# One layer of a hybrid SSD and S5 encoder: angle tables made per batch, another form of the S5 GELU, and a new order of the instructions

## The chip, the cores and the metric

The kernel runs on one core of a Trainium2 chip. The time is the device time of one execution in microseconds (us). Work goes to five engines, each with its own queue of instructions that it works through in order: TensorE (PE, matrix products), VectorE (DVE), ScalarE (ACT, functions through tables), GpSimd (POOL) and SyncE (SP), which here only starts transfers.

## What is computed

One inference step of one layer, for 1024 prompt frames and 32 frames of a running stream with its own states. Both share one set of weights; the width is 1024.

```python
xn = rmsnorm(x, pre_mix_norm_w)
z, xbc, dt_raw, u_s5 = split(xn @ w_in)                  # 512 | 1024 | 8 | 512 columns
y_ssd = ssd_mixer(z, xbc, dt_raw, ...)                   # causal conv, SiLU, chunked scan, gate, norm
# s5_mixer: 32 groups of 16 channels, each a diagonal complex state of 64
dt = exp(log_dt); ang = lam_im * dt; mag = exp(lam_re * dt)
lb = mag * (cos(ang) + i sin(ang))                       # the step of the scan
h  = associative_scan(lb, B u, start=h0)
y  = Re(C h) + d * u
g  = gelu(y, approximate=True) @ glu_w + glu_b           # per group
y_s5 = g[..., :16] * sigmoid(g[..., 16:])
h  = x + rmsnorm(concat(y_ssd, y_s5) @ w_out, post_mix_norm_w)
up = causal_dwconv(rmsnorm(h, pre_ffn_norm_w) @ w_up)    # 5632 columns
gate, val = split(up)
y  = h + rmsnorm((gelu(gate) * val) @ w_down, post_ffn_norm_w)
```

Outputs are y and the new states and conv histories of both streams, in float32.

## The kernel before

The 1056 columns (frames) lie in the free dimension, the features on the 128 partitions. Block 0 is 512 columns, block 1 is 544, worked in two chunks of 272. The large products are made of three passes in a reduced format that together carry the accuracy of float32: high weight by high input, high weight by low input, low weight by high input (`pm` is the PSUM tile). Weights come as tiles of 128 by 1024 (`raw`, 512 KB each). For each, ACT writes the high part (`wh`, line 566, which is the line of a helper that holds all of ACT's operations), and DVE the rest (`wl`, line 745). Two buffers each hold `raw`, `wh` and `wl`. The line of nearly all matmuls is 510, of the transposes 514.

The stages: the first norm (its per-column factor is made by a chain of small DVE operations, lines 634 to 657, on tiles `nrt`, `nry`, `nra`; it is spread over the partitions through `scr` and a product with ones), the projection `w_in`, then SSD and S5 side by side with the stream of weights, `w_out`, and the feed-forward part: `up_evac` reads PSUM into `fext` (lines 1771 and 1773, DVE), the convolution and GELU follow, and the second product collects in `acc` (line 1843). At the end of each block, `fin_mm` and `fin_out` make the last norm. `apply` (lines 1932 to 1946) treats a chunk in four pairs of 128-feature rows: each is multiplied by the norm's factor (line 1939, `acc<-acc,sacc`) and the residual is added (line 1945 from `hr` in block 0, line 1942 from `o` in block 1). The tuple `fp` names, per chunk, the pairs whose multiplication (and, for block 0 and the first chunk of block 1, addition) goes to POOL instead of DVE.

S5 goes in 8 batches of four groups; a column there is 132 slots of 8 frames each (528 elements for four groups). For each batch:

- `s5_prep` makes products of parameters on POOL (`outer`, line 1129: `gz`, `gt` and the W tiles; `gz` is the sum of two products, line 1134). PE uses `gz` in a product with `ck`, whose result goes through DRAM to `Traw` and `Tg`, and in transposes, which ACT copies to `GT`. It also makes the angle tables TC (cosine) and TS (sine) of the slots: ACT scales the slot numbers to turns, DVE takes off whole turns (lines 1143 to 1146, and `wrap`, 931 and 932), ACT takes Sin. Two batches share this: the even batch (`u == 0`) makes the turns for both, one batch on each half of the partitions, in `yr`; each batch takes Sin on its half and sends the copies to the other half by three transfers.
- `s5_run` makes the input products, turns them with TC and TS into `rr`, scans (R), and turns back into `hq` (line 1212 on POOL, 1213 on DVE).
- `s5_out` makes the output product of three terms in PSUM, its GELU by the tanh formula (Copy and Square from PSUM on ACT, an operation on DVE, Tanh on ACT, an operation on DVE), and the GLU.

ACT holds one set of function tables at a time: by the kernel's own list, Silu and Sin are in one, Gelu_apprx_tanh in another, Exp in a third; where the set changes, an ACT_TABLE_LOAD stands in its queue.

The order of the instructions on each engine is set ahead of the run by a class `Plan`. It reads all instructions and what each depends on (`read`, `buffers`), gives each a duration (`cost`), and makes a list schedule: on each engine, of those that are ready, the one of the best rank comes first (`schedule`). Ranks come from `ROUND` passes backward and forward (`rounds`), then each seed in `NUDGES` shifts the ranks of some instructions in a stretch at random, one after the other (`nudge`). The orders of the last pass are fixed with dependencies. So a new constant or a new seed can move any instruction of any engine.

## Time and profile before

| what | us |
|---|---|
| median of three runs | 1260.25 |
| range of the three runs | 1259.05 to 1261.12 |
| the profiled execution | 1260.22 |
| its span, first to last instruction | 1258.4 |
| busy: PE, DVE, ACT, POOL | 1225.7, 1004.5, 573.0, 409.1 |
| mean granted PE clock, share of full speed | 0.980 |
| first matmul starts, last one ends | 1.24, 1250.3 |

Busy time says how full an engine is. A wait on PE shows as idle time in front of an instruction, and its releaser is the instruction of another engine that ended it. The clock that PE is granted is given as a share of 2.4 GHz; at 0.50 every matmul takes twice as long.

### The profile page before, as it was taken

What the parts mean: (1) busy time and instruction counts of PE and PEld (TensorE: products, weight loads), DVE (VectorE), ACT (ScalarE), POOL (GpSimd) and SP (SyncE); (2) the same over time, 40 slices, a digit from 0 to 9 for tenths busy, and PEclk for the clock granted to TensorE, in tenths of its full rate; (3) what the DMA queues carried; (4) which work ended last, traced back from release to release, by engine and by line L of the source; (5) the groups of instructions that cost most, each with busy time, mean ns of one, the idle gap of its engine ahead of it and who ended that gap; (6) DMA issues with size and microseconds to landing.
All of it is one profiled execution on the core that took longest, in us unless ns stands there. A gap on an engine that the chain in (4) does not pass through costs nothing.

```text
span 1258.4 us, 20994 instructions
## 1 busy us (share of the span) xinstructions
PE 1225.7 (97%) x7885; PEld 1105.9 (88%) x7885; DVE 1004.5 (80%) x1755; ACT 573.0 (46%) x967; POOL 409.1 (33%) x574
## 2 busy tenths in 40 slices
PE   9999999999998999999999999998999999999995
PEld 7879989998887887878987888898999999999994
DVE  6788877898979898887698987778676777776777
ACT  8246655564545554543454433362532333333343
POOL 3484555363156333221453311126110111111013
PEclk7899989999999999999999999999999999999997
DMA  7154434243346322333433432223322232322212
GB/s 242 39 156 128 117 87 133 82 125 103 100 125 205 117 93 76 117 131 108 137 112 102 142 101 87 98 85 125 110 85 84 84 101 85 101 85 84 85 54 72
DMA packets 68821, 135.39 MB, mean 108 GB/s; under 512 B 14320, under 2 KB 35184, under 8 KB 68720
## 3 DMA queue, kind: packets, MB, share of 16 engines
q1 hardware_dynamic: 68720, 134.05, 34.0%
q8 instruction: 62, 1.02, 0.3%
q14 instruction: 39, 0.32, 0.1%
HBM read 111.69 MB, written 15.81 MB: 101 GB/s over the span
## 4 chain that ended last, share of the span: by engine, by line
PE 84%; DVE 5%; issue 1%; DMA 1%; ACT 1%; POOL 0%; SPq 0%; DVEq 0%; ACTq 0%; POOLq 0%
PE pm L510 75%; PE ms L510 9%; PE ms L514 1%; DVE o L1707 1%; DVE wl L745 1%; DVE acc L1939 0%; DMA raw<-wt 0%; DVE xl L1710 0%; ACT L566 0%; DMA kd<-s5d 0%; SPq L1190 0%; DVE acc L1942 0%; DVE sp L1335 0%; DMA gluw<-glu 0%; DVE acc L1945 0%
## 5 line engine op out<-in xcount | busy, mean ns | idle before, releaser
L510 PE MATMUL pm<-xh,wh 128*128 128x272 f32 (+1 forms) x1616 | 527.6, 329 | 3.5 <-DVE fext L1771 2.2
L510 PE MATMUL pm<-xh,wl 128*128 128x272 f32 (+1 forms) x1616 | 526.4, 329 | 4.1 <-DVE wl L745 4.1
L510 PE MATMUL pm<-xl,wh 128*128 128x272 f32 (+1 forms) x1616 | 527.5, 327 | 2.0 <-DVE xl L1710 1.9
L510 PEld LDWEIGHTS pm<-xh,wh 128*128 128x128 f32 x1616 | 306.6, 190 | 26.8 <-issue 3.1
L510 PEld LDWEIGHTS pm<-xh,wl 128*128 128x128 f32 x1616 | 305.6, 190 | 27.7 <-DVE wl L745 5.3
L510 PEld LDWEIGHTS pm<-xl,wh 128*128 128x128 f32 x1616 | 306.9, 190 | 24.2 <-DVE xl L1710 2.3
L566 ACT ACTIVATE wh<-raw 128x1024 fp32r<-128x1024 f32 x120 | 126.6, 1056 | 153.8 <-PE pm L510 133.1
L510 PE MATMUL pm<-al,dh 128*128 128x272 f32 (+1 forms) x528 | 170.4, 325 | 0.0
L510 PE MATMUL pm<-ah,dh 128*128 128x272 f32 (+1 forms) x528 | 169.3, 326 | 1.0 <-ACT acc L566 0.8
L510 PE MATMUL pm<-ah,dl 128*128 128x272 f32 (+1 forms) x528 | 168.3, 323 | 0.0
L745 DVE TENSOR_TENSOR wl<-raw,wh 128x1024 fp32r<-128x1024 f32 x120 | 157.5, 1314 | 13.4 <-ACT wh L566 13.0
L1843 DVE TENSOR_TENSOR acc<-acc,pm 128x272 f32<-128x272 f32 (+1 forms) x232 | 119.2, 521 | 51.0 <-PE pm L510 49.5
L1788 DVE SCALAR_TENSOR_TENSOR ftmp<-fext,vec_t,ftmp 128x512 f32<-128x512 f32 (+1 forms) x176 | 141.3, 804 | 13.1 <-ACT ftmp L566 11.1
L1766 POOL COPY fext<-halo 128x2 f32<-128x2 f32 x88 | 41.9, 476 | 298.7 <-DVE ftmp L1788 281.2
L1771 DVE TENSOR_TENSOR fext<-pm,rbc 128x512 f32<-128x512 f32 (+2 forms) x132 | 67.2, 511 | 74.4 <-PE pm L510 73.5
L566 ACT ACTIVATE ftmp<-fext,vec_t 128x512 f32<-128x512 f32 (+1 forms) x88 | 72.4, 824 | 83.3 <-DVE fext L1773 40.3
L510 PEld LDWEIGHTS pm<-ah,dh 128*128 128x128 f32 x528 | 99.0, 188 | 9.1 <-ACT acc L566 1.0
L510 PEld LDWEIGHTS pm<-al,dh 128*128 128x128 f32 x528 | 99.3, 188 | 7.2 <-issue 0.3
L510 PEld LDWEIGHTS pm<-ah,dl 128*128 128x128 f32 x528 | 98.6, 188 | 7.3
L566 ACT ACTIVATE dh<-raw 128x1024 fp32r<-128x1024 f32 (+1 forms) x46 | 46.7, 1020 | 75.1 <-PE pm L510 62.5
L1821 DVE TENSOR_TENSOR dl<-raw,dh 128x1024 fp32r<-128x1024 f32 (+1 forms) x46 | 56.7, 1235 | 7.1 <-ACT dh L566 7.1
L566 ACT ACTIVATE ftmp<-ftmp 128x512 f32<-128x512 f32 (+1 forms) x44 | 28.1, 639 | 70.9 <-DVE ftmp L1788 70.9
(323 smaller groups left out, 1659.0 us busy)
## 6 DMA issues: line engine op xcount, KB each, us to landing
raw<-wt SPq DMA_DIRECT2D x164, 512.0 KB, 3.3
gluw<-glu SPq DMA_DIRECT2D x8, 512.0 KB, 3.6
xst<-xT SPq DMA_DIRECT2D x16, 136.0 KB, 3.2
pbd<-pbo SPq DMA_DIRECT2D x8, 272.0 KB, 2.5
xr<-xT SPq DMA_DIRECT2D x8, 272.0 KB, 3.1
pbi<-pbd SPq DMA_DIRECT2D x8, 272.0 KB, 2.9
yT<-acc SPq DMA_DIRECT2D x8, 272.0 KB, 2.2
ud<-uext SPq DMA_DIRECT2D x4, 528.0 KB, 2.9
```

Of the source, the lines that this page charges most:

```text
L510: PE.matmul(out, lhsT, rhs, start=start, stop=stop, **kw)
L514: PE.transpose(out, in_, ident)
L566: S.activation(out, in_, func, bias=bias, scale=scale)
L745: V.tensor_tensor(lo, r, hi.bitcast(F32), sub)
L1707: V.scalar_tensor_tensor(h, h, vc("post_mix", k), r1, mult, mult)
L1766: G.tensor_copy(e[:, 0:2], halo[:, j, :])
L1771: V.tensor_tensor(e[:, 2 + o:2 + o + wp], ps[:, :wp], rbc[:, t0:t0 + wp], mult)
L1788: V.scalar_tensor_tensor(t, e[:, i:i + n], vc("fw", 3 * j + i), t, mult, add)
L1821: V.tensor_tensor(l, rr, h.bitcast(F32), sub)
L1843: V.tensor_tensor(a, a, ps[:, :w], add)
```

## The change

Four parts.

1. The angle tables are made batch by batch, on all 128 partitions: turns, wrap, Sin for TS, Abs and Sin for TC. The three transfers per batch, the constant `nsgn2pi` and four small copies into `dt5` go. Per pair of batches there are now 8 scaled copies, 4 Sins and 2 Abs on ACT (before 4, 5 and 1), and twice as many operations for turns and wrap on DVE.
2. The GELU of the S5 output is one ACTIVATE, Gelu_apprx_tanh from PSUM. Two ACT operations and two DVE operations of each batch go in part or whole: both Copies, both Squares and the Tanh on ACT become two Gelus, and the two DVE operations are gone. The factor 2 that the tanh form left in is taken out of the GLU's scales (0.25 becomes 0.5).
3. `fp` gives one pair of the first chunk of block 1 back to DVE.
4. In `cost` three estimates change, and ROUND and NUDGES are new (ROUND 7 with 33 seeds, now 6 with 56).

In the order of the changed kernel there are 7297 matmuls as before, 1771 DVE operations (before 1757), 974 on ACT (969), among these 35 table loads (22), 577 on POOL (579), and 481 transfers (505).

```diff
 PAR = dict(...
-           fp=((1, 3), (1, 3), ()),
+           fp=((1, 3), (3,), ()),
...
-ROUND, NUDGES = 7, (12, 19, 34, 43, 47, 57, 66, 73, 88, 96, 149, 160, 173, 180, 187, 210, 250, 257, 276, 376, 383,
+ROUND, NUDGES = 6, (14, 35, 47, 59, 82, 112, 125, 149, 188, 206, 225, 233, 269, 353, 368, 418, 536, 595, 612, 651,
...
         elif e == "Pool":
             self.shared[q] = len(big) > 1
-            d = 0.21 + 0.00165 * n if len(big) > 1 else 0.17 + 0.0009 * n
+            d = 0.21 + 0.0021 * n if len(big) > 1 else 0.17 + 0.0009 * n
         else:
-            self.shared[q] = not ps and n > 8
+            self.shared[q] = not ps
...
-                wire = max(wire, s + 0.9) + self.bytes[q] / 280e3
+                wire = max(wire, s + 0.9) + self.bytes[q] / 380e3
...
-        for k, n in enumerate(("f8a", "f8b")):
-            for hf in range(2):
-                q = slice(64 * hf, 64 * hf + 64)
-                V.tensor_copy(dt5[q, 16 * k:16 * k + 16].rearrange("p (i g) -> p i g", g=4),
-                              small[n][q].rearrange("p (i h g) -> p i h g", h=2, g=4)[:, :, hf])
...
-        if u == 0:
-            yy = small["yy"] = tl("tytr", [128, 2, 4, NCH5], "yr")
-            y, t = yy[:, 0], yy[:, 1]
-            f8 = small["dt5"]
-            for g in range(4):
-                act(y[:, g], cs("slot"), AF.Copy, scale=f8[:, 2 * i + g:2 * i + g + 1])
-            V.tensor_scalar(t, y, MAGIC, MAGIC, add, sub)
-            V.tensor_tensor(y, y, t, sub)
-            for g in range(4):
-                V.scalar_tensor_tensor(y[:, g], cs("slot"), f8[:, 16 + 2 * i + g:17 + 2 * i + g], y[:, g], mult, add)
-            wrap(y, t)
-            act(t, y, AF.Abs)
-            act(t, t, AF.Sin, scale=-TWOPI, bias=cs("halfpi"))
-        y, t = small["yy"][:, 0], small["yy"][:, 1]
-        me, other = (slice(64 * v, 64 * v + 64) for v in (u, 1 - u))
-        act(TSn[me], y[me], AF.Sin, scale=cs("sgn2pi")[me])
-        act(y[me], y[me], AF.Sin, scale=cs("nsgn2pi")[me])
-        D.dma_start(TSn[other], y[me])
-        D.dma_start(TC[me], t[me])
-        D.dma_start(TC[other], t[me])
+        y = tl("tytr", [128, 4, NCH5], "yr")
+        for g in range(4):
+            act(y[:, g], cs("slot"), AF.Copy, scale=small["f8a"][:, 4 * i + g:4 * i + g + 1])
+        V.tensor_scalar(TC, y, MAGIC, MAGIC, add, sub)
+        V.tensor_tensor(y, y, TC, sub)
+        for g in range(4):
+            V.scalar_tensor_tensor(y[:, g], cs("slot"), small["f8b"][:, 4 * i + g:4 * i + g + 1], y[:, g], mult, add)
+        wrap(y, TC)
+        act(TSn, y, AF.Sin, scale=cs("sgn2pi"))
+        act(y, y, AF.Abs)
+        act(TC, y, AF.Sin, scale=-TWOPI, bias=cs("halfpi"))
...
-        sq = th
...
-            act(y[:, 2 * b:2 * b + 2], pv, AF.Copy)
-            act(sq[:, 2 * b:2 * b + 2], pv, AF.Square)
-        V.scalar_tensor_tensor(sq, sq, 1.0 / GC1, y, add, mult)
-        act(th, sq, AF.Tanh, scale=GC0 * GC1)
-        V.scalar_tensor_tensor(gg, th, 1.0, y, add, mult)
+            act(gg[:, 2 * b:2 * b + 2], pv, AF.Gelu_apprx_tanh)
...
-                act(th[:, k], ps[1][:, o], AF.Tanh, scale=0.25, bias=gb_t[:, 4 * i + k, 1:2])
-                act(yq[:, k], ps[0][:, o], AF.Identity, scale=0.25, bias=gb_t[:, 4 * i + k, 0:1])
+                act(th[:, k], ps[1][:, o], AF.Tanh, scale=0.5, bias=gb_t[:, 4 * i + k, 1:2])
+                act(yq[:, k], ps[0][:, o], AF.Identity, scale=0.5, bias=gb_t[:, 4 * i + k, 0:1])
```

In the listings of the order the lines of the changed kernel differ from those of before: 1129 and 1134 became 1125 and 1130, 1212 became 1199, 1939, 1942 and 1945 became 1921, 1924 and 1927, 1771 became 1753, and the lines of the small chain and of `wl` are one higher.

POOL, near 165 us, where an S5 batch is prepared (`gz`, `gt`) while the batch ahead runs (`hq`, `fin`); `xb` and `o` are small copies of the SSD part. Before:

```order
L818 COPY o_73<-xb_90 128x3
L804 COPY xb_90<-xb_89 128x3
L1212 TENSOR_TENSOR hq<-R_1855,TS 128x4x132
L1215 COPY fin_107<-hq 128x4x4
L1216 COPY hq<-sml 128x8
L1129 TENSOR_TENSOR gz<-pq,bb 128x512
L1134 TENSOR_TENSOR gz<-gz,gt 128x512
L1129 TENSOR_TENSOR gt_2067<-pq,bcr 128x512
```

and now:

```order
L819 COPY o_73<-xb_90 128x3
L805 COPY xb_90<-xb_89 128x3
L1125 TENSOR_TENSOR gz<-pq,bb 128x512
L1130 TENSOR_TENSOR gz<-gz,gt 128x512
L1125 TENSOR_TENSOR gt_2053<-pq,bcr 128x512
L1199 TENSOR_TENSOR hq<-R_1846,TS 128x4x132
L1202 COPY fin_107<-hq 128x4x4
L1203 COPY hq<-sml 128x8
```

The pair of `gz` operations and a `gt` stood behind `hq` and its two copies, and now stand ahead of them.

DVE, near 870 us, where block 0 ends (`acc` is its result, `hr` the residual) and the feed-forward part of block 1 has begun (`fext` reads PE's result, `wl` is the low part of the next weights). Before:

```order
L1939 TENSOR_TENSOR acc_4899<-acc_4899,sacc 128x1024
L1771 TENSOR_TENSOR fext<-pm,rbc 128x272
L1945 TENSOR_TENSOR acc_4899<-acc_4899,hr 128x512 x2
L1771 TENSOR_TENSOR fext<-pm,rbc 128x240
L1771 TENSOR_TENSOR fext<-pm,rbc 128x272
L1771 TENSOR_TENSOR fext<-pm,rbc 128x240
L745 TENSOR_TENSOR wl<-raw,wh 128x1024
L1939 TENSOR_TENSOR acc_4899<-acc_4899,sacc 128x1024
L1945 TENSOR_TENSOR acc_4899<-acc_4899,hr 128x512
L745 TENSOR_TENSOR wl<-raw,wh 128x1024
L1773 TENSOR_TENSOR fext<-pm,rbc 128x32 x2
```

and now:

```order
L1770 SCALAR_TENSOR_TENSOR ftmp<-fext,vec_t,ftmp 128x546 x2
L1780 TENSOR_TENSOR ftmp<-ftmp 128x546
L1753 TENSOR_TENSOR fext<-pm,rbc 128x272
L1753 TENSOR_TENSOR fext<-pm,rbc 128x240
L1921 TENSOR_TENSOR acc_4883<-acc_4883,sacc 128x1024
L1927 TENSOR_TENSOR acc_4883<-acc_4883,hr 128x512 x2
L1755 TENSOR_TENSOR fext<-pm,rbc 128x32
L1753 TENSOR_TENSOR fext<-pm,rbc 128x272
L746 TENSOR_TENSOR wl<-raw,wh 128x1024
L1921 TENSOR_TENSOR acc_4883<-acc_4883,sacc 128x1024
L1927 TENSOR_TENSOR acc_4883<-acc_4883,hr 128x512 x2
```

Before, one `fext` read of 272 columns stood ahead of the first two additions and three reads behind them; now a read of 272 and one of 240 stand ahead of the multiplication and its additions, and the next three follow behind a `wl`.

DVE, at the very end: the applications of the pairs of the first chunk of block 1 (`acc` with `sacc`, `acc` with `o`) and the chain of the last norm. Before:

```order
L1907 TENSOR_TENSOR sacc<-sacc,osq 128x272
L1939 TENSOR_TENSOR acc_8893<-acc_8893,sacc 128x2x272
L1942 TENSOR_TENSOR acc_8893<-acc_8893,o_6246 128x2x272
L634 TENSOR_SCALAR nrt<-ms_13121 128x2
L634 TENSOR_SCALAR nrt<-ms_13121 16x1
L637 TENSOR_SCALAR nry<-nrt 128x3
L651 TENSOR_TENSOR nra<-nry 128x3
L652 SCALAR_TENSOR_TENSOR nra<-nra,nrt 128x3
L653 SCALAR_TENSOR_TENSOR nry<-nra,nry 128x3
L1939 TENSOR_TENSOR acc_8893<-acc_8893,sacc 128x2x272
```

and now:

```order
L1889 TENSOR_TENSOR sacc<-sacc,osq 128x272
L1921 TENSOR_TENSOR acc_8877<-acc_8877,sacc 128x2x272
L1924 TENSOR_TENSOR acc_8877<-acc_8877,o_6230 128x2x272
L635 TENSOR_SCALAR nrt<-ms_13105 128x2
L1921 TENSOR_TENSOR acc_8877<-acc_8877,sacc 128x2x272
L1924 TENSOR_TENSOR acc_8877<-acc_8877,o_6230 128x2x272
L635 TENSOR_SCALAR nrt<-ms_13105 16x1
L638 TENSOR_SCALAR nry<-nrt 128x3
L652 TENSOR_TENSOR nra<-nry 128x3
L653 SCALAR_TENSOR_TENSOR nra<-nra,nrt 128x3
```

Before, one pair stood ahead of the chain and half of another within it; now two pairs stand ahead of it, with one of the chain's operations between them.

## Rows read from the trace of the kernel before

**Rows 1.** Page, busy time of each engine (us, share of the span, instructions).

```profile
PE 1225.7 (97%) x7885; PEld 1105.9 (88%) x7885; DVE 1004.5 (80%) x1755; ACT 573.0 (46%) x967; POOL 409.1 (33%) x574
```

**Rows 2.** Waits of PE: waiting line, releaser, us in total, times, longest.

```profile
PE pm L510 <- DVE wl L745: 4.1, 3, 1.8
PE pm L510 <- DVE fext L1771: 2.2, 1, 2.2
PE pm L510 <- DVE xl L1710: 1.9, 1, 1.9
PE ms L510 <- POOL gz L1134: 1.9, 1, 1.9
...
PE pm L510 <- ACT wh L566: 1.1, 2, 0.7
```

**Rows 3.** Windows: length, busy PE, PEld, DVE, ACT, POOL, then clock, DMA, GB/s.

```profile
168.20:175.00 6.80, 6.55 (x24) 5.97 (x25) 4.99 (x9) 2.88 (x6) 2.83 (x4) 0.50 0.62 183
...
874.70:878.20 3.50, 3.50 (x18) 3.50 (x18) 3.47 (x5) 0.00 (x0) 3.50 (x5) 0.51 0.60 184
```

**Rows 4.** Windows, 100 to 300 us in four parts: busy us, the sum.

```profile
sum 200.00, PE 197.49 PEld 182.42 DVE 168.44 ACT 119.30 POOL 103.37; mean PE 49.37 PEld 45.60 DVE 42.11 ACT 29.82 POOL 25.84
```

**Rows 5.** ACT by form, 75 to 300 us: busy us, mean ns, idle before, releasers.

```profile
L566 ACT ACT_TABLE_LOAD x8 | 10.3, 1283 | 0.1
...
L566 ACT ACTIVATE y5s<-ms 128x264 f32<-128x264 f32 x16 | 6.3, 391 | 20.1 <-PE ms L510 19.6 <-DVE sp L1335 0.5
...
L566 ACT ACTIVATE ge<-ge 128x528 f32<-128x528 f32 x8 | 5.1, 642 | 2.1 <-DVE ge L1239 2.1
...
L566 ACT ACTIVATE yr<-cst_t,sml 128x132 f32<-128x132 f32 x12 | 4.3, 398 | 6.6 <-issue 4.2 <-DMA ug<-ud 2.1 <-DMA TS<-yr 0.3
```

**Rows 6.** Timeline of ACT (start, length, engine, line, operation, names, shapes).

```profile
105.11 1.28 ACT L566 ACT_TABLE_LOAD   x1
106.41 0.65 ACT L566 ACTIVATE ge<-ge 128x528 f32<-128x528 f32 x1
```

**Rows 7.** DVE by form, 75 to 300 us.

```profile
L1239 DVE SCALAR_TENSOR_TENSOR ge<-ge,y5s 128x528 f32<-128x528 f32 x8 | 8.8, 1096 | 3.6 <-ACT ge L566 3.6
L1241 DVE SCALAR_TENSOR_TENSOR ge<-ge,y5s 128x528 f32<-128x528 f32 x8 | 7.3, 913 | 0.1
...
L1168 DVE TENSOR_TENSOR kd<-kd 32x64 f32<-32x64 f32 x8 | 2.7, 336 | 3.2 <-DMA TS<-yr 1.7 <-DMA TC<-yr 0.7 <-DMA raw<-wt 0.4
```

**Rows 8.** Timeline of POOL, 160 to 172 us (in brackets: idle before, releaser).

```profile
162.47 1.33 POOL L1212 TENSOR_TENSOR hq<-R,TS 128x528 f32<-128x528 f32 x1 [2.73 <-ACT y5s L566]
...
165.68 1.05 POOL L1129 TENSOR_TENSOR gz<-pq,bb 128x512 f32<-128x512 f32 x1
166.81 1.59 POOL L1134 TENSOR_TENSOR gz<-gz,gt 128x512 f32<-128x512 f32 x1
```

**Rows 9.** Timelines of POOL, DVE and PE, 68 to 82 us.

```profile
71.54 1.29 POOL L1134 TENSOR_TENSOR gz<-gz,gt 128x512 f32<-128x512 f32 x1
...
68.77 4.22 DVE L1146 SCALAR_TENSOR_TENSOR yr<-cst_t,sml,yr 128x132 f32<-128x132 f32 x4
...
73.50 0.96 PE L510 MATMUL ms<-ck,gz 128*128 128x16 f32 x8
...
78.34 0.61 PE L510 MATMUL ms<-ug,GT 128*128 128x132 f32 x4
```

**Rows 10.** Timeline of DVE, 868 to 880 us.

```profile
867.66 4.23 DVE L1945 TENSOR_TENSOR acc<-acc,hr 128x512 f32<-128x512 f32 x2
```

**Rows 11.** Timelines of DVE and PE, the last 22 us.

```profile
1241.42 1.74 DVE L1942 TENSOR_TENSOR acc<-acc,o 128x544 f32<-128x544 f32 x1
...
1245.88 1.18 DVE L653 SCALAR_TENSOR_TENSOR nry<-nra,nry 128x3 f32<-128x3 f32 x1
...
1247.80 0.16 DVE L655 SCALAR_TENSOR_TENSOR nra<-nra,nrt 128x3 f32<-128x3 f32 x1
...
1249.00 1.27 PE L510 MATMUL ms<-scr,ones_r 128*128 128x272 f32 x2 [7.04 <-DVE scr L670]
```

More of the change, by code (lines that the diff above doesn't have):

```diff
@@ L50 @@
            run3=0.5, uload=6.619, swap_pool=1, z_s5=1, ssd0=13.784, ssd1=0.0, ssd2=2.778, gate0=76.032, glu0=0.384, glu1=2.807, abufs=2,
-           cvat='run7', tcat=1, late_at=2, nsq=1, fg=(), fp=((1, 3), (1, 3), ()), fch=(0, (0, 1), 2), pfin=0, q0=0, q1=0, q2=0, nb=0,
+           cvat='run7', tcat=1, late_at=2, nsq=1, fg=(), fp=((1, 3), (3,), ()), fch=(0, (0, 1), 2), pfin=0, q0=0, q1=0, q2=0, nb=0,
            hv=(), av=(3,), post0=0.802, dn_at=((3, 0), (3, 1)), ob_at=22, sa=2, sb=1, y5b=0, cvb=2.11, msb=(1, 1, 2, 2, 2), pch0=(3,),
@@ L67 @@
 for _name, _w in (("ident", 128), ("upper", 128), ("lstrict", 128), ("slot", NCH5), ("open", NCH5), ("tau", 16),
-                  ("sgn2pi", 1), ("nsgn2pi", 1), ("halfpi", 1), ("sel", 8)):
+                  ("sgn2pi", 1), ("halfpi", 1), ("sel", 8)):
     CST[_name] = (_n, _n + _w)
@@ L89, in shape_constants @@
     put("sgn2pi", np.where(i < 64, TWOPI, -TWOPI)[:, None])
-    put("nsgn2pi", np.where(i < 64, -TWOPI, TWOPI)[:, None])
     put("halfpi", np.pi / 2)
@@ L182 @@
 DMA_LANES = 8
-ROUND, NUDGES = 7, (12, 19, 34, 43, 47, 57, 66, 73, 88, 96, 149, 160, 173, 180, 187, 210, 250, 257, 276, 376, 383,
-                   481, 527, 539, 546, 554, 624, 685, 858, 912, 971, 1073, 1079,)
+ROUND, NUDGES = 6, (14, 35, 47, 59, 82, 112, 125, 149, 188, 206, 225, 233, 269, 353, 368, 418, 536, 595, 612, 651,
+                   695, 723, 757, 812, 874, 949, 988, 1036, 1097, 1196, 1239, 1321, 1355, 1390, 1429, 1464, 1476,
+                   1571, 1581, 1629, 1639, 1679, 1702, 1784, 1802, 1865, 1881, 1947, 1959, 1980, 1999, 2072, 2084,
+                   2153, 2196, 2207,)
 class Plan:
```

## The prediction

> **What bounds the kernel now.** I read the page's busy line first. TensorE (PE) is busy 1225.7 us of a span of 1258.4 [rows 1]: every other engine matters only where PE ends up waiting for it. So the second view is the list of PE's waits: not a share but single places, three for `wl` (4.1 in all), one each for `fext` (2.2), `xl` (1.9) and `gz` (1.9) [rows 2], and the largest, 7.04 us for `scr`, at the very end [rows 11]. The third view is the granted clock by stretch, because a wait costs more than itself: behind the `gz` wait PE ran 6.8 us at a clock of 0.50, behind the `fext` wait 3.5 us at 0.51 [rows 3]. 0.50 is 1.2 of the 2.4 GHz, so these stretches cost another 3.4 and 1.7 us. In both PE had just stood still for about 2 us. The fourth view is the stage in which the S5 batches run beside the weight stream, 100 to 300 us: of 200 us PE is busy 197.5, VectorE (DVE) 168.4, ScalarE (ACT) 119.3, GpSimd (POOL) 103.4 [rows 4]. ACT has 80.7 us without work there, DVE 31.6. An edit that adds work there costs nothing as long as it does not stand, in an engine's fixed order, ahead of something that PE is about to need.
>
> The profiled execution took 1260.2 us (1.8 around its span), the median of the three runs is 1260.25; I make the sum against 1260.2.
>
> **GELU of the S5 output.** Per batch it removes two Copies from PSUM (0.391 us each, 16 in all), one Tanh (0.642, 8) on ACT, and two DVE operations (1.096 and 0.913) [rows 5, 7]. The Square from PSUM becomes Gelu_apprx_tanh on the same tile; I take it at the Copy's 0.391. But Gelu needs another table than Sin and Silu, and the order of the changed kernel has 35 table loads where before there were 22, the 13 new ones in the S5 stage: 13 x 1.283 = 16.7 us of ACT [rows 5]. The trace shows a load of 1.28 us and the next ACTIVATE 0.02 us behind it [rows 6], so I charge 1.283 and no more. The angle tables add 16 Copies of 0.398 on ACT; their 4 more Abs and 4 fewer Sins about cancel. Net on ACT: 16.7 - 8 x 0.642 - 16 x 0.391 + 16 x 0.398 = +11.7 us, into 80.7 us of idle time. What hides it: before each S5 output ACT stands waiting for PE's result (the idle time before the Copies: 20.1 us for 16 of them [rows 5]), and a load needs nothing from PE, so it runs in that wait. And the chain from PSUM to the GLU's input loses ACT, DVE, ACT, DVE in sequence and becomes one ACTIVATE: 0.642 + 1.096 + 0.913 = 2.65 us shorter. What if the cover is gone: a load stands in ACT's queue ahead of a `wh` split or a `GT` copy that PE needs, and PE waits up to 1.28. Bounds: 16.7 (all on the path) and a gain of some us (the shorter chain was late somewhere; but no PE wait for `ge` is in the list). I take +1.0, nearly one load that lands on PE, since 13 loads lie beside 80.7 us of idle time.
>
> The Trainium skill, ScalarE: Activation LUTs, section What ACT_TABLE_LOAD costs, speaks against this edit: it gives a switch of the table set as about 1283 ns of load and another 1380 ns of drain, 2.66 us. The load agrees with this trace to the nanosecond; the drain is not seen in it. By the page ACT's addition would be 13 x 2.66 = 34.6 us instead of 16.7, an estimate, and still inside the idle time.
>
> **Angle tables batch by batch.** DVE loses 16 operations of the GELU (8 x 1.096 + 8 x 0.913 = 16.1) and gets 16 `yr` operations on a quarter of the columns and 16 on all of them. Even at the 1.096 of the longest row here for each (35.1) that is +19.0 us, into 31.6 of idle time [rows 4, 7]. Zero on the path. 24 transfers between the halves of the partitions go; DVE's `kd` operation waited for them 1.7 + 0.7 us [rows 7], on an engine with time to spare. I credit nothing; bounds 0 and -2.4.
>
> **The redrawn order.** The new planner constants and seeds move everything, so I go through PE's large waits, in order of time, and ask of the new order what stands there.
>
> Start: the `xst` loads stand ahead of the first weight tile on SP's queue now. The first split comes a little later; no row prices it, and I put +0.5 (bounds 0 and 1.5).
>
> Near 45 us: one of the three `wl` waits, the longest, 1.8 [rows 2]. In the new order this `wl` comes directly behind the small operations of the norm that moved ahead. I expect 0.4 of wait to be left: -1.4.
>
> First S5 batches: here the new order is worse. On POOL one `gt` and two W products stand ahead of the first `gz` where one `gt` stood: two operations more of the kind that takes 1.05 us [rows 8]. The `gz` pair ended at 72.83 and PE used it at 73.50 [rows 9], so 0.7 of the 2.1 is covered: +1.4. And DVE puts all eight `pq` operations and a `wl` ahead of the angle chain (the 4.22 us row), whose Sins stand ahead of the `GT` copies on ACT. I count some 3.7 us of DVE work moved in front; `GT` ends later by about that, and PE used it at 78.34, just when it was there [rows 9]. The first 1.4 us of waiting covers a part, the `kd` work about 0.5 more: +1.8, together +3.2; bounds 0 (the parameters are ready earlier) and +7 (the clock falls too).
>
> The `gz` wait near 168 us: before, POOL takes the pair of `gz` operations behind an `hq` product of the batch ahead, which itself stood still for 2.73 us [rows 8]. In the new order `gz`, `gz` and `gt` come first. They then wait only for PE to have read the former `gz`, and between that and PE's next use lie 4.5 us of matmuls, against 1.05 + 1.59 us of POOL work [rows 8]. `hq` comes some 3 us later, but PE's use of it also moved, by 2.5 us, and had time. I take the wait off whole and the slow stretch with it: -1.9 - 3.4 = -5.3; bounds 0 and -5.3.
>
> Near 390 us: `xl` 1.9 and another `wl` [rows 2]. DVE is full there, in the new order with about 1 us less of other work between the same weight tiles. PE's own work there shrinks too by 0.7: -0.6; bounds 0 and -3.
>
> Near 870 us: `fin_out` of block 0. Two `hr` additions take 4.23 us on DVE beside POOL's own [rows 10], and the `fext` reads that PE waits for stand behind them in the order. In the new order one 272 and one 240 read stand ahead of these additions. The wait was 2.2 for `fext` and 1.0 for the `wl` behind, with 1.7 from the clock: 4.9 in all [rows 2, 3]. The `wl` still stands behind additions: I take half, -2.5; bounds 0 and -4.9.
>
> Tail: PE's 7.0 us for `scr` is DVE's chain of ten small operations, some of which take 1.18 while POOL works on SBUF beside them, and 0.16 when it does not [rows 11]. With one pair less on POOL (the change of `fp`) POOL is done before the chain begins, and DVE does the second pair ahead of it. I count from 1240.7: 2.5 for the first pair (its second half took 1.74 beside POOL), 1.9 for the second, ten operations at 0.2 with their gaps, `scr` 0.5. `scr` ends at 1247.6; PE went on at 1249.00 [rows 11]. -1.4; bounds +1 (all of the chain slow again) and -2.5.
>
> An allowance: a new order brings places of its own that the old one didn't have. The old one has four such waits near 2 us. I take one, like `xl` (1.9) with a stretch like the one at 874.7 (1.7): +3.6; bounds 0 and two of them.
>
> **Sum.** +1.0 + 0 + 0.5 - 1.4 + 3.2 - 5.3 - 0.6 - 2.5 - 1.4 + 3.6 = -2.9. 1260.2 - 2.9 = 1257.3 us.
>
> **Rivals.** (a) The freed time comes back: what is late next in each place (the `hq` behind `gz`, the `wl` behind `hr`) is as late as what was freed. For it: PE is busy 97%, and the waits lie where several engines are late together. Half of -5.3, -2.5, -1.4 and -0.6 (9.8 in all) is given back: 1260.2 - 2.9 + 4.9 = 1262.2 at the most, 1260.3 if the allowance is one of them. (b) Slower, by table loads: three or four of the 13 stand in ACT's queue right ahead of a `wh` or a `GT` that PE needs; each costs 1.28 and a half-clock stretch of 1.7. Without the GELU term of the forecast I have 1256.3, and 3.5 x 2.98 = 10.4 more: 1266.7. It becomes slower than before from two loads on (1256.3 + 2 x 2.98 = 1262.3). Against it: with 22 loads PE's waits for `wh` are 1.1 us in all [rows 2]. (c) The same place, but a switch costs two loads' time, 2.57, because the engine empties first: 1256.3 + 3.5 x (2.57 + 1.7) = 1271.2. The two rows of a load and its successor speak against it [rows 6]. The page named above is the one that says so. (d) Better: the new order has no place of its own, the first batches are ready in time, and the `fext` wait goes whole: 1257.3 - 3.6 - 2.4 = 1251.3. That the edits don't do what they say is excluded by the new order, which shows them.
>
> **How the numbers follow.** Forecast 0.46, with its own range 1254 to 1260.5; (a) 0.18, (b) 0.17, (c) 0.04, (d) 0.15. A measurement of this kernel can tell about 0.2% from no change: 2.5 us, so faster is under 1257.7, slower over 1262.8. The forecast lies close to the border: of its 0.46 I give 0.27 to faster and 0.18 to same. With (d) and a little of (a): faster 0.44; same 0.33; slower 0.23, mostly (b). The range 1250.5 to 1265.5 leaves out the lower part of (d), 0.06, and (c) with the upper half of (b), 0.13.
>
> **What would show it.** In the profile after: no PE wait for `gz` near 165 us and a full clock there; the tail's `scr` wait at 5.5 to 6; a shorter `fext` wait at the change of blocks; 35 table loads of 1.28 us, and no `wh`, `GT` or `ge` wait over 1 us on PE in 100 to 300 us. A PE wait for `gz` or `GT` in 70 to 80 us would confirm the price of the first batches. Wrong I am if PE waits for ACT in the S5 stage (b), or if a half-clock stretch stands where none was, at a place that I haven't named.

## The result, and the profile after

The changed kernel takes 1274.53 us (median of 4 runs, 1274.22 to 1274.91), the kernel before 1259.65 beside it: ratio 1.0124, 95% interval 1.0106 to 1.0143. It is slower by 14.9 us where I had forecast a gain of 2.9, and outside the range. The profiled execution took 1274.36, its span 1272.6 us (before 1258.4).

The page's busy line and PE's waits, largest first (to be held against [rows 1, 2]):

```profile
PE 1232.4 (97%) x7885; PEld 1107.7 (87%) x7885; DVE 1012.7 (80%) x1769; ACT 583.6 (46%) x972; POOL 408.7 (32%) x572
```

```profile
PE pm L511 <- DVE wl L746: 6.1, 5, 3.0
PE ms L511 <- DVE scr L671: 5.7, 1, 5.7
PE pm L511 <- ACT wh L567: 5.1, 3, 3.1
PE pm L511 <- DVE uext L791: 4.6, 2, 4.3
PE pm L511 <- DVE fext L1755: 3.3, 1, 3.3
PE pm L511 <- DVE zst L847: 2.1, 1, 2.1
```

ACT got 10.6 us more work (forecast 11.7), DVE 8.2. The `gz` wait of [rows 2] is gone, the tail's `scr` wait shorter. New are `uext`, `zst` and a `wh` of 3.1; `fext` and `wl` have grown. Next the windows of PE by stage, first of the kernel before, then of the changed one (length, busy time, granted clock, DMA share, GB/s):

```profile
0.00:40.00 40.00, 37.51 (x180) 0.83 0.60 191
40.00:60.00 20.00, 18.20 (x106) 0.83 0.14 50
60.00:110.00 50.00, 47.82 (x331) 1.00 0.50 138
110.00:300.00 190.00, 187.49 (x1309) 0.98 0.40 111
300.00:350.00 50.00, 50.00 (x324) 1.00 0.35 103
350.00:430.00 80.00, 75.95 (x440) 0.98 0.48 156
...
850.00:910.00 60.00, 56.01 (x430) 0.97 0.37 121
```

```profile
0.00:40.00 40.00, 35.58 (x158) 0.79 0.61 191
40.00:60.00 20.00, 18.71 (x117) 0.91 0.08 29
60.00:110.00 50.00, 44.47 (x278) 0.93 0.38 114
110.00:300.00 190.00, 190.00 (x1364) 1.00 0.36 103
300.00:350.00 50.00, 47.89 (x299) 0.97 0.29 91
350.00:430.00 80.00, 72.10 (x411) 0.94 0.44 150
...
850.00:910.00 60.00, 55.55 (x383) 0.94 0.31 106
```

I count as lost, in each stretch, PE's idle time plus half the length of what ran at a clock of 0.50 (110 to 300 before: 2.5 idle and 3.4 of clock). The first two columns belong to the result. The other four are kernels without picked moves, told of below. There the sum agrees with the spans only within some 3 us; between before and after it does within 0.2. Each column is of one profiled execution: those of n_consts and n_edits took 1263.5 and 1264.3 us, 2.1 and 4.5 less than their medians, so these two columns show less than the medians further down.

| us lost in | before | after | n_before | n_consts | n_edits | n_after |
|---|---|---|---|---|---|---|
| 0-40 | 9.3 | 12.9 | 7.6 | 12.0 | 5.5 | 12.9 |
| 40-60 | 5.2 | 3.0 | 5.7 | 4.6 | 5.7 | 1.3 |
| 60-110 | 2.2 | 8.9 | 1.9 | 0.7 | 6.8 | 11.7 |
| 110-300 | 5.9 | 0 | 0.7 | 1.1 | 0.5 | 0 |
| 300-350 | 0 | 3.8 | 0 | 0.7 | 0 | 3.6 |
| 350-430 | 5.7 | 13.0 | 13.9 | 11.8 | 14.1 | 12.9 |
| 430-850 | 0 | 0.1 | 3.9 | 0 | 1.4 | 1.0 |
| 850-910 | 5.7 | 7.9 | 5.7 | 6.8 | 7.3 | 8.5 |
| tail (`scr`) | 7.0 | 5.7 | 6.5 | 6.2 | 5.0 | 5.0 |

Between before and after the differences sum to +14.3. Two places gained about what I had forecast (40 to 60, tail), 110 to 300 gained 5.9, and five lost 23.6. The rows behind four of these, as timelines of after (start, length, engine, line, operation; idle time in brackets). The start, SP's queue and ACT:

```profile
1.19 1.37 SPq L1074 DMA_DIRECT2D xst<-xT  x3
2.60 0.43 SPq L734 DMA_DIRECT2D raw<-wt  x1
...
8.58 1.06 ACT L567 ACTIVATE wh<-raw 128x1024 fp32r<-128x1024 f32 x1 [0.56 <-DMA raw<-wt]
```

Three `xst` stand ahead of the first weight tile (`raw`) where one stood; its split `wh` starts at 8.58 instead of 5.71. The tile's transfer is issued 0.94 us later and takes 6.0 us to land where it took 4.0. The first S5 batches, DVE:

```profile
67.13 3.48 DVE L1029 TENSOR_SCALAR pq<-LRI 64x256 f32<-64x256 f32 x5
70.64 0.65 DVE L791 TENSOR_TENSOR uext<-pm,rbc 128x272 f32<-128x272 f32 x1
71.13 1.48 DVE L746 TENSOR_TENSOR wl<-raw,wh 128x1024 fp32r<-128x1024 f32 x1
```

Five `pq` products stand ahead of the `uext` that empties the PSUM tile PE needs. The norm between the blocks, DVE, and the change of blocks near 884 us (which answers to [rows 10]):

```profile
392.15 8.72 DVE L1689 SCALAR_TENSOR_TENSOR o<-o,vec_t,oacc 128x512 f32<-128x512 f32 x6
...
407.60 3.43 DVE L1692 SCALAR_TENSOR_TENSOR xl<-o,vec_t,xh 128x512 fp32r<-128x512 f32 x2
410.95 2.28 DVE L746 TENSOR_TENSOR wl<-raw,wh 128x1024 fp32r<-128x1024 f32 x1
```

```profile
880.08 3.30 DVE L1921 TENSOR_TENSOR acc<-acc,sacc 128x1024 f32<-128x1024 f32 x1
883.41 4.57 DVE L1927 TENSOR_TENSOR acc<-acc,hr 128x512 f32<-128x512 f32 x2
887.90 0.18 DVE L1755 TENSOR_TENSOR fext<-pm,rbc 128x32 f32<-128x32 f32 x1
```

From 395.7 us on, beside POOL, the `o` and `xl` operations on DVE take 1.75 to 1.79 us each (two just ahead of these took 0.74), and the `wl` that PE waits for comes behind them. Near 884 a `fext` of 0.18 us waits behind 7.9 us of one multiplication and two additions. (In the second DVE listing ahead of the prediction this read of 32 columns and one of 272 stand behind the additions and ahead of the `wl`, not behind a `wl` as the sentence under it says.)

### The profile page after: what moved, and what is told of

Read it like the earlier page. It is cut to its first block, busy times and chain, and to the rows that moved or that the text cites. A ratio compares the mean times of both kernels' runs of the same rounds, so it can differ in the third digit from the quotient of the medians.

```text
span 1272.6 us, 20984 instructions
## 1 busy us (share of the span) xinstructions
PE 1232.4 (97%) x7885; PEld 1107.7 (87%) x7885; DVE 1012.7 (80%) x1769; ACT 583.6 (46%) x972; POOL 408.7 (32%) x572
## 4 chain that ended last, share of the span: by engine, by line
PE 90%; DVE 6%; DMA 2%; ACT 1%; issue 1%; SPq 0%; DVEq 0%
PE pm L511 79%; PE ms L511 10%; DVE wl L746 1%; DVE acc L1921 1%; PE ms L515 1%; DVE o L1689 1%; DMA raw<-wt 0%; DMA z<-zd 0%; DVE uext L791 0%; DMA ud<-uext 0%; DVE acc L1924 0%; DVE pq L1029 0%; DVE ftmp L1770 0%; DVE xl L1692 0%; ACT wh L567 0%
## 5 line engine op out<-in xcount | busy, mean ns | idle before, releaser
L1770 DVE SCALAR_TENSOR_TENSOR ftmp<-fext,vec_t,ftmp 128x512 f32<-128x512 f32 (+1 forms) x176 | 138.4, 787 | 6.9 <-ACT ftmp L567 4.9
```

The source lines that it names most:

```text
L1770: V.scalar_tensor_tensor(t, e[:, i:i + n], vc("fw", 3 * j + i), t, mult, add)
```

## The experiments

Theory O: the redrawn order made the loss, the edits as such cost next to nothing. Theory E: the edits made it, through table loads and DVE's longer angle work. Where gains by place are given, they come from comparing when PE starts its k-th product of a large weight tile into `pm` (6432 of them in each kernel), in one profiled execution of each.

**The edits in the old order.** The order of the kernel before was written out, and one edit or both put in.

```diff
 e_gelu:  -act(y, pv, Copy); act(sq, pv, Square); V.stt; act(th, sq, Tanh); V.stt
          +act(y, pv, Gelu_apprx_tanh)                   # GLU scales 0.25 -> 0.5
 e_angle: -if u == 0: y, t of a pair of batches ... + 3 transfers
          +y of each batch ..., V.tensor_scalar(TC, y, MAGIC, ...)
 e_both:  both
```

> The kernel before with the GELU edit alone: Gelu_apprx_tanh straight from PSUM, into the tile that the Copy filled, and the Copy, Square, Tanh and two DVE operations gone; every other instruction keeps its place in the order of the kernel before. 33 table loads instead of 22. Theory O (the redrawn order made the loss, the edits cost next to nothing): 1257 to 1261 us, within 0.2% of before, and no PE wait for ACT over 1 us in 100 to 300 us that before did not have. Theory E (the edits made it, by table loads ahead of work that PE needs and by half-clock stretches behind them): 1266 or more.

> The kernel before with the angle tables made batch by batch, and no transfers between the halves; the GELU as before and every other instruction in its place in the order of the kernel before (the chain of each second batch is put a few us ahead of the place where its Sin stood). Theory O: 1258 to 1262. Theory E: 1264 or more, by a PE wait for Tg or GT in 70 to 200 us, since DVE gets 19 us more work there.

> Both edits, in the order of the kernel before. Theory O: 1257 to 1262, some 12 us or more under the changed kernel, which has the same two edits in its own order. Theory E: 1270 or more, close to the changed kernel's 1274.5.

e_gelu: 1255.9 us, ratio 0.9976 (0.9964 to 0.9988), a gain of 3.3. e_angle: 1282.4, 1.0197 (1.0172 to 1.0222). e_both: 1281.0, 1.0190 (1.0167 to 1.0214). So the GELU edit alone is faster, with 33 table loads, and theory E is out for it. POOL in e_gelu, against [rows 8]:

```profile
158.27 1.34 POOL L1427 TENSOR_TENSOR hq<-R,TS 128x528 f32<-128x528 f32 x1 [2.73 <-ACT ge L781]
...
161.49 1.06 POOL L1344 TENSOR_TENSOR gz<-pq,bb 128x512 f32<-128x512 f32 x1
162.63 1.61 POOL L1349 TENSOR_TENSOR gz<-gz,gt 128x512 f32<-128x512 f32 x1
```

`hq` still stands ahead of `gz` and still waits 2.73 us, but it starts at 158.27 instead of 162.47, and PE's wait for `gz` and the slow stretch behind it are gone (6.0 us between the 450th and the 600th product). The rows name ACT as what `hq` waits for, the results of the GLU. But `hq` is the product of the scan R with TS, and it starts 0.13 us behind the end of DVE's scan in both kernels, while the ACT operation named in [rows 8] had ended 0.33 us earlier. So the wait has to be followed through DVE. The kernel before, then e_gelu:

```profile
155.38 0.63 ACT L566 ACTIVATE xb<-xo 128x512 f32<-128x512 f32 x1
156.89 1.54 DVE L809 SCALAR_TENSOR_TENSOR xo<-xb,vec_t,xo 128x512 f32<-128x512 f32 x2 [3.50 <-ACT xo L566]
...
161.08 1.26 DVE L1210 TENSOR_TENSOR_SCAN R<-M,rr 128x528 f32<-128x528 f32 x1
```

```profile
151.04 0.63 ACT L781 ACTIVATE xb<-xo 128x512 f32<-128x512 f32 x1
152.56 1.54 DVE L1024 SCALAR_TENSOR_TENSOR xo<-xb,vec_t,xo 128x512 f32<-128x512 f32 x2 [0.51 <-ACT xo L781]
...
156.88 1.26 DVE L1425 TENSOR_TENSOR_SCAN R<-M,rr 128x528 f32<-128x528 f32 x1
```

Before, DVE stood still for 3.50 us until ACT had done `xb` and `xo` of the SSD part, which stand in ACT's queue behind the batch's Copy, Square, Tanh and four table loads (145.7 to 155.4 us, without a gap). In e_gelu there are three loads and two Gelus, ACT comes to `xb` 4.3 us earlier, and DVE's `xo` and R, POOL's `hq` and `gz` all come 4.2 to 4.3 us earlier. (The two profiled executions differ by 6.0 us, the medians by 3.3.) For the angle tables theory O missed by 20 us: PE waits for `rr` and `xb` on DVE (7.7 and 10.8 in e_both). In part that was my placing: the rounding step writes into TC, which the `hq` of the batch two ahead still reads, and DVE stood still for it.

```diff
 k_both2 (on e_both):
-y = tl("tytr", [128, 4, NCH5], "yr");     V.tensor_scalar(TC, y, MAGIC, ...); wrap(y, TC)
+yy = tl("tytr", [128, 2, 4, NCH5], "yr"); V.tensor_scalar(t, y, MAGIC, ...);  wrap(y, t)
```

> Both edits in the order of the kernel before, as e_both, with one thing more: the rounding step of the angle chain writes into the free half of its own tile instead of the cosine table TC, so that it doesn't wait for the hq of the batch two ahead to have read TC. In e_both four operations of the chain stood up to 15 us later in DVE's order for that reason, ahead of rr and xb that PE waited for. Theory T (that wait was the cost): 1256 to 1265, and PE's waits for rr and xb in 80 to 240 us (4.2, 2.6, 5.8, 3.1, 2.5 us in e_both) are gone. Theory D (DVE's additional work was the cost, wherever it stands): 1272 or more.

1271.6, ratio 1.0097 (1.0071 to 1.0123): between the two. The wait for TC was 9.4 us of it by the medians (11.7 by the ratios). The rest stands: an `rr` wait of 4.2 and `xb` waits of 2.6, 3.3 and 1.8, each behind the second batch's chain. With the chains at these places, the order drawn for the old program has no room for the angle edit; other places were not tried. Does the converse hold?

```diff
 u_angle (on after, in after's order):
-y of each batch ...
+if u == 0: y, t of a pair of batches ... + 3 transfers, 3 us ahead of the first one's place
```

> The changed kernel with the angle tables made in pairs of batches again, as in the kernel before; GELU, constants and the order of everything else as in the changed kernel (the chain of a pair, now one instead of two, stands 3 us ahead of the place of the first one's, since its tables still have to go through transfers). Theory A (after the first runs: it is the angle edit that costs; DVE does the whole chain of operations on 528 columns twice as often, and the redrawn order could hide most of it but not all): 1262 to 1270, with less lost in 60 to 100 us. Theory O (the redrawn order alone loses the time that the GELU edit gained): 1272 to 1277.

1285.3, ratio 1.0209 (1.0184 to 1.0235): 10.8 slower still. Neither theory gave that. Taking this edit out of an order drawn for it costs 10.8, and putting it into one that wasn't cost 12 and more. Such transplants price the misfit, not the edit.

**The angle work taken away without a move.**

```diff
 c_angle8 (on after, after's order; batches with u == 1 only)
-V.tensor_scalar(TC, y, ...); V.tensor_tensor(y, y, TC, sub); 4 V.stt; wrap(y, TC)   # 528 columns
+the same on [:, :, :2]                                                             # 8 columns
```

> The changed kernel in its own order, with the DVE operations of every second batch's angle chain done on 8 of 528 columns (their input set to zero): it leaves out half of the angle tables, so its output is wrong, and DVE gets about the work of the kernel before for them. Nothing else moves. Theory A (the angle edit's work on DVE is what PE waits for): less is lost in 60 to 110 us, 3 us or more, and little elsewhere since PE loses only 0.7 us in 110 to 270; 1268 to 1271. Theory O (the places that lose time, at the start, 66, 326, 390 to 420 and 884 us, have no instruction of either edit; the order does it): within 2 us of the changed kernel, 1272.5 to 1275.

1275.3, ratio 1.0130 (1.0111 to 1.0148); all five places as in the changed kernel. In this order the columns that the angle tables add on DVE are not what PE waits for. Theory A is out, O holds; the edit's work on ACT and the number of its DVE operations stay in this run, so it shows nothing of them.

**The order of the changed kernel repaired.**

```diff
 r_all
 SP  -vec_t xst xst xst raw ...         +vec_t xst raw xst xst ...
 ACT -xh xh xh wh                       +xh wh xh xh
 DVE -pq x5, uext, wl                   +uext, wl, pq x5
 DVE -y*z (waits for z), zst            +zst, y*z
 DVE -o x6 xl o xl o xl x2 wl xl x4 wl  +o x4 xl x2 o xl wl o x2 xl x2 wl o xl x3
 DVE -hr x2, fext, fext, wl             +fext, hr, fext, wl, hr
```

> The changed kernel with 27 of its instructions put elsewhere in its order, at the five places where its PE waits or half-clock stretches are new or larger: at the start (the small load of raw ahead of the second xst, the first wh ahead of the second xh), at 66 (uext and wl ahead of five pq products), at 326 (zst ahead of a y*z that waits for a DMA), at 390 to 420 (the o, xl and wl operations in the sequence that the kernel before has), at 884 (fext ahead of the two hr additions). The edits stay. Theory O: these places hold 10.8 us of PE's standing still and about as much again of half clock that the kernel before does not have; 1253 to 1260, as fast as before or faster. Theory E: the waits turn up elsewhere, 1268 or more. A third (P): the order is to blame, but the engines that are late at these places are full, so that the waits move a little further down: 1262 to 1268.

1274.6, ratio 1.0135: no gain. (The kernel moves 25 instructions, not 27.) By place: `zst` -2.8. The start gained 2.6 at the first product, and by 64 us 4.5 was lost again: now `wl` stood behind three `xl` on DVE (PE waited 3.4 for it) and the slow stretch came anyway. Near 400: -2.5, then +6.3. `fext`: -2.9, then +2.0 by a `wl` and an `acc`. That is theory P but for `zst`. The next two repaired more.

```diff
 r_all2: start, with wl ahead of the second xl; zst; fext; nothing near 400;
         60-85 as in before: DVE uext, wl and 4 pq first, other 4 pq behind the angle chain;
         POOL gz ahead of W; ACT M behind GT
 r_all3: start and zst as in r_all2; near 400 both DVE and POOL in before's sequence
         POOL -o x5 pacc x3 o x3 pacc x3   +o x4 pacc x2 o pacc o x2 pacc x2 o pacc
```

> The changed kernel with a fuller repair of its order at four places, and none at 390 to 420. Start: as in r_all, and the first wl ahead of the second xl on DVE (in r_all it stood behind three xl, and PE waited 3.4 us for it). First batches: on DVE uext, wl and the four pq products that gz needs first, the other four behind the angle chain; on POOL gz ahead of the W products; the M copies on ACT behind GT: the sequences of the kernel before. zst and fext as in r_all, where PE stood 2.8 us and about 1 us less. Theory O: 2.5 to 3 at the start, 3 to 5 in 60 to 100 us, 2.8 and 1 more: 1262 to 1267. Theory P (the engines are full at the start and in the first batches, so that the wait moves on as it did in r_all): 1268 to 1274.

> The changed kernel with its order repaired at the start (as in r_all2, which gained 2.4 us there) and for zst (2.8 to 3.9 us), and at 390 to 420 us with both engines in the sequence of the kernel before: DVE's o, xl and wl as in r_all, and now POOL's o and pacc too (r_all left POOL's as they were, and lost 6 us behind 415, where POOL did three pacc at the end). Theory O: the loss at 390 to 430 falls from 11.7 us to about the 6.3 of the kernel before; with the other two 1262 to 1266. Theory C (DVE and POOL are both full there and slow each other; the sequence matters little): the loss there stays at 9 or more, 1267 to 1271.

r_all2: 1270.0, ratio 1.0089 (1.0060 to 1.0118). r_all3: 1271.5, 1.0100 (1.0081 to 1.0119). `zst` stayed mended in both, about 3 us net. The first batches gained 5.1 and lost 5.6 a little later, to the second batch's `gz`. PE in r_all2:

```profile
83.72 0.40 PE L529 MATMUL ms<-ck,gz 128*128 128x16 f32 x2 [2.75 <-POOL gz L1148]
```

Near 400 in r_all3 the `wl` wait of 3.0 became a `wh` wait of 3.8: ACT's `wh` stands behind an `xr` that waits for POOL.

```profile
403.92 0.63 ACT L582 ACTIVATE xr<-o 128x512 f32<-128x512 f32 x1 [2.80 <-POOL o L1705]
```

The loss from 390 to 430 us is 11.6 there, and 11.9 in the changed kernel. So theory O holds for `zst`, P at 66 us, C near 400. At the start O holds in small part only, and what is kept goes with the clock: the same edit kept 1.6 us by the 75th product in r_all2 and 0.2 in r_all3, where the first slow stretch was 6.8 us long and not 3.4.

**POOL's share near 400 us.**

```diff
 c_nopacc (on after, after's order; block 0)
-G.tensor_tensor(pacc, pacc, xr[:, kk], add)               # 512 columns
+G.tensor_tensor(pacc[:, :8], pacc[:, :8], xr[:, kk, :8], add)
```

> The changed kernel, same order, with POOL's six pacc additions of block 0 in 403 to 420 us done on 8 of 512 columns: it leaves out most of one sum of squares, so its output is wrong; some 8 us less work for POOL beside DVE. Theory C (at 390 to 420 us DVE is late because its o and xl operations take 1.75 us beside POOL and 0.74 alone; POOL is busy 19.7 of the 20 us there, 9.8 in the kernel before): the operations beside the former pacc take 0.74, the loss there falls from 11.7 to 6 or less, 1267 to 1270. Theory O (the place of wl in DVE's order, behind ten o and xl operations, is the cost): PE still waits 3 us for wl, 1273 or more.

1270.5, ratio 1.0092 (1.0066 to 1.0117): -4.0, of it 3.5 at this place. The `wl` wait of 3.0 is gone; the others there stay. DVE in c_nopacc, first beside POOL's `o`, then beside its `pacc` of 8 columns:

```profile
403.81 1.78 DVE L1903 SCALAR_TENSOR_TENSOR o<-o,vec_t,oacc 128x512 f32<-128x512 f32 x1
405.52 0.74 DVE L1906 SCALAR_TENSOR_TENSOR xl<-o,vec_t,xh 128x512 fp32r<-128x512 f32 x1
406.18 0.74 DVE L1903 SCALAR_TENSOR_TENSOR o<-o,vec_t,oacc 128x512 f32<-128x512 f32 x1
```

Theory C holds, for some half of the 7.3 us that the changed kernel loses more there. From 400 to 420 us POOL is busy 19.7 us in the changed kernel, 13.9 in the same stretch of c_nopacc and 15.0 in that of the kernel before (393 to 413; the 9.8 in my expectation is of 400 to 420, where that kernel is some 7 us further on). Why the other half is lost stays open: less work for POOL than before does not bring it back, nor does the sequence of the kernel before (r_all3).

**Who drew this order?** ROUND as in each kernel, the list of picked moves empty.

```diff
 n_before / n_after: -NUDGES = (12, 19, ...) / (14, 35, ...)   +NUDGES = ()
 n_consts (on n_before), the reverse for n_edits (on n_after):
-0.21 + 0.00165 * n; shared = not ps and n > 8; bytes / 280e3
+0.21 + 0.0021 * n;  shared = not ps;           bytes / 380e3
 n_angle   (on n_before): +angle tables batch by batch
 n_noangle (on n_after):  -angle tables batch by batch
```

> The changed kernel without its picked moves (the list of seeds empty), constants and edits as they are: the order that the planner's rounds give by themselves. Theory L (each drawn order has its own unlucky places; the picks decide over as much as the whole loss): 1280 to 1295, with large waits at other places than the changed kernel's, so that the 56 picks gained 5 to 20 us and still fell short of the old kernel's. Theory K (the refitted constants or the edits make every order slower, the picks matter little): 1272 to 1278.

> The kernel before without its picked moves: theory L: 1268 to 1290, some 10 to 30 us above the kernel before's 1259, so that the two kernels without picks differ less than, or otherwise than, the two with them. Theory K: 1258 to 1264, and n_after stays 10 or more above it.

> The kernel before without picked moves (1261.4), with the three refitted constants of the changed kernel's planner and nothing else: POOL's price for operations on two large operands up from 0.00165 to 0.0021 us a column, small DVE operations on SBUF counted as sharing with POOL, a transfer's wire time at 380 instead of 280 KB/us. The planner orders otherwise, and no instruction is different. Theory K1 (the refitted constants are the cause): 1270 to 1276, with PE waiting 3 us for wh at the start (raw behind three xst), 4 to 5 for uext near 66 us and about 2 for zst near 327, as with and without picks in the changed kernel. Theory K2 (the edits, by the order that they lead the planner to): 1259 to 1265 and none of these.

> The changed kernel without picked moves (1272.2), with the three constants of the kernel before: all edits, old prices. K1: 1255 to 1264, without the waits at the start, near 66 and near 327 us. K2: 1270 to 1276, with them. If both matter, each of the two kernels lies between, and their sum tells.

> The kernel before without picked moves (1261.4), with the angle tables made batch by batch and nothing else of the change; the planner orders the new program by its old constants. Of the edits' +7.4 us (n_edits against n_before) this shows the angle tables' part. Theory T (it is the angle tables: DVE gets more operations in the S5 stage and the planner has to put other work elsewhere for them): 1266 to 1271, with new PE waits for dt, GT or gz in 80 to 200 us and larger ones in 390 to 410. Theory G (it is the GELU edit's table loads, which the planner prices at 4.0 us a switch where a load takes 1.28): 1260 to 1263.

> The changed kernel without picked moves (1272.2) and without the angle edit: GELU edit, tail edit and refitted constants stay, and the planner orders the new program. Theory T (the angle tables make the orders slower, the GELU edit doesn't): 1264 to 1268, about n_consts (1265.6) less 1 for the tail. Theory G (the GELU edit does it through its table loads): 1270 to 1274, with the waits near 66 and 327 us still there. n_angle put the angle tables at +3.6 of the edits' 7.4 with the old constants, so a value between, 1268 to 1270, says that both do.

| no picked moves | us | ratio to before (95%) |
|---|---|---|
| n_before | 1261.4 | 1.0021 (1.0009-1.0034) |
| n_consts | 1265.6 | 1.0042 (1.0024-1.0059) |
| n_angle | 1265.0 | 1.0041 (1.0023-1.0058) |
| n_edits | 1268.8 | 1.0074 (1.0050-1.0099) |
| n_after | 1272.2 | 1.0106 (1.0083-1.0130) |
| n_noangle | 1274.2 | 1.0121 (1.0101-1.0141) |

Theory L falls: n_after has the waits of the changed kernel (`wh` 3.1, `uext` 5.0, `zst` 1.9, `fext` 5.0), so the picks did not make them; only near 400 PE waits for another operand (4.1 us for ACT's `E`, not 3.0 for `wl`). K holds: without picks the two kernels are 10.8 us apart. By the medians the constants alone give +4.1, the edits alone +7.4, and both at once 10.8. n_before and n_after were timed together, n_consts and n_edits on another chip; by the ratios, each to the kernel before beside it, the steps are 2.6, 6.7 and 10.7 us, and the intervals of n_before and n_consts overlap. In n_consts no instruction is different, so what it loses is the order's. In n_edits the instructions differ too, and whether they or their order cost the 7.4 no run separates. (It has ROUND 6 and n_before 7; the planner draws the same order for it with either.) The start comes from the constants: `wh` waits 3.5 us in n_consts and 0.3 in n_edits. PE's waits in n_consts:

```profile
PE pm L509 <- DVE fext L1770: 5.0, 1, 5.0
PE pm L509 <- ACT wh L565: 4.9, 3, 3.5
```

The picks make up the rest: the old ones gained 2.6 us (1261.4 to 1258.8), the new ones lost 2.3 (1272.2 to 1274.5; by the ratios the intervals overlap). These are medians of different sessions, so with the 10.8 they come to 15.7 and not to 14.9. In the table above the old picks are worth 8 us at 350 to 430 alone; every order without them in that table loses 12 to 14 there, and the new ones left that as it was. Which edit costs the 7.4 stays open: the angle tables alone give +3.6 (2.5 by the ratios, where the intervals of n_before and n_angle overlap), but without them the changed kernel isn't faster (n_noangle), it has an `rr` wait of 3.8 at 190 us instead. The parts don't add up, since each run is another order. (My expectation for n_angle is wrong on one point: the planner charges 1.3 us for a table load; the 4.0 only says how far it holds back an operation of another table.)

**A version that beats both.**

```diff
 e_best (on e_gelu): fp of the changed kernel; in before's order, on DVE
 -nrt x4, 8 small, wl    +wl, nrt x4, 8 small           (45 us)
 -y*z, zst               +zst, y*z                      (316 us)
 -hr, hr, fext x3, wl    +hr, fext x3, wl, hr           (862 us)
 e_best2 (on e_best): that wl ahead of the first of them, the next wl in its place
```

> The kernel before with the GELU edit (e_gelu, 1255.9) and the changed kernel's tail (one pair of additions moved from POOL to DVE), in the order of the kernel before, with three places mended: wl ahead of the small operations of the norm at 45 us (there e_gelu loses 1.6 and 3.4 of half clock), zst ahead of the y*z that waits for a transfer (1.1), and three fext and a wl ahead of the second hr addition at 862 us (3.2 and 3.4 of half clock). If the places are independent: tail -1.4, -2 to -5, -1, -2 to -5: 1245 to 1250. If the waits move on, as most did in the repairs of the changed kernel: 1252 to 1256.

> As e_best, with the two wl near 860 us put further ahead on DVE: one into the 2.4 us in which DVE waits for PE, the other ahead of the second hr. In e_best PE waited 0.7 and 2.8 us for them. If DVE has that room: 1249 to 1252. If the hr additions, which come later, make the next fext or ftmp late: no change, 1252.5 to 1254.5.

e_best 1253.5, ratio 0.9956 (0.9938 to 0.9973): the place at 45 us gave 2.5 and `zst` 1.2, and both held; `fext` 1.3, of which 0.9 came back; the tail only 0.45. These gains are from an execution of 1250.0 us, 3.5 below the median, so they are rather too large. e_best2 1252.7, 0.9951 (0.9933 to 0.9970): no different, a `fext` waits again.

```profile
PE pm L725 <- DVE fext L1983: 3.2, 1, 3.2
```

Of a hoped-for 6 to 11 us below e_gelu some 2.4 to 3.2 came. Both are faster than the kernel before by intervals clear of 1; against e_gelu (0.9964 to 0.9988) their intervals overlap, so the places mended are not shown to add to it.

## Why the prediction was wrong, point by point

- **GELU** (+1.0): wrong sign in the old order, where it gains 3.3; what it is worth in the new one no run shows. My cover argument for the loads held: in after 35 loads of 1.283 us, and in 100 to 300 us PE idles for none of them.

```profile
109.40 1.28 ACT L567 ACT_TABLE_LOAD   x1
110.70 0.39 ACT L567 ACTIVATE ge<-ms 128x264 f32<-128x264 f32 x1
```

```profile
sum 200.00, PE 200.00 PEld 183.96 DVE 173.69 ACT 124.04 POOL 101.91; mean PE 50.00 PEld 45.99 DVE 43.42 ACT 31.01 POOL 25.48
```

 The step that failed was "no PE wait for `ge` is in the list", with ACT's idle time taken as a whole. The shorter chain freed ACT's queue for `xb` and `xo`, and through DVE's scan R and POOL's `hq` it brought `gz` forward by 4.2 us, which is PE's wait near 168. Following that wait back, engine by engine, would have shown it; [rows 8] alone names ACT rightly as the end of the chain, but not as what `hq` waits for. Behind the load the Gelu starts after 0.02 us; the Trainium skill's drain of 1380 ns (ScalarE: Activation LUTs, What ACT_TABLE_LOAD costs) is not in this trace either.
- **Angle tables** (0): c_angle8 shows nothing lost by their columns on DVE in the changed kernel. That holds in an order drawn with them: in the old order the two edits together cost some 12 us (k_both2), and drawing an order for the angle tables alone gave 2.5 to 3.6 more (n_angle). I had compared their work with idle time and not asked what the planner would move for them.
- **Start** (+0.5, measured +3.6): mis-sized, upper bound 1.5. One step is in SP's queue (`raw` issued at 2.60 instead of 1.66), but it lands 2.9 us later: two more `xst` are ahead of it in transfer. I had priced the issue alone. In r_all, with `raw` and `wh` moved forward, the next operand was late: `wl`, behind `xl` on DVE.
- **45 us** (-1.4, measured -2.2): held.
- **First batches** (+3.2, measured +6.7): sign and place right, mechanism wrong. PE waited neither for `gz` nor `GT`, but for a `uext` and a `wl` behind the `pq` block. I had counted what those eight `pq` delay on the angle chain, not who empties PSUM behind them.
- **`gz` at 168** (-5.3, measured -5.9): right in size, but the GELU edit alone brings it in the old order.
- **390** (-0.6, measured +7.3): wrong sign, the largest miss. I compared the amount of other work between weight tiles. What I left out is that DVE's `o` and `xl` take more than twice their length beside POOL's, and that POOL is busy nearly all the time there. That is 3.5 us (c_nopacc); the cause of the other half stays open.
- **870** (-2.5, measured +2.2): I saw a 272 and a 240 read go ahead of the additions and missed the 32-column one that stayed behind.
- **Tail** (-1.4, measured -1.4): right with its mechanism. PE's `scr` wait is 5.68 against 7.04 in [rows 11]; POOL is done at 1259.51, and the chain of small operations begins at 1260.77 and takes 0.14 to 0.17 us for each.

```profile
1263.13 1.27 PE L511 MATMUL ms<-scr,ones_r 128*128 128x272 f32 x2 [5.68 <-DVE scr L671]
```

- **Allowance** (+3.6): one new place was right in itself (`zst`, +3.8). But I had read three of the other terms as gains or nothing, and there too the new order was worse.
- **Rivals**: none was the cause. (b) named the right side for a wrong reason: PE has no wait for ACT in 110 to 300 us. (a), waits that come back, is what ate the repairs r_all to r_all3.

The failure common to 390, 870 and the first batches: I judged each place by the wait that it had before, and asked whether the new order removes that one. That is the step of the sum that failed: -0.6, -2.5 and +3.2 were to come from these three places, and they gave +7.3, +2.2 and +6.7. An order drawn anew has to be searched for the waits it makes: for each of PE's operands, what stands ahead of its producer.
